# Attention in a hybrid layer: key and query halves through memory, values in two groups, one transpose for the maxima

## The chip, the cores and the metric

The kernel runs on one core of one Trainium2 chip. The metric is the time of one execution in microseconds (us). A core has five engines with a queue each: TensorE (PE, matrix products; its weight loads are shown apart as PEld), VectorE (DVE), ScalarE (ACT), GpSimdE (POOL) and SyncE (SP, which here issues every DMA). Each queue is worked off in order, and an instruction that waits for another engine or a transfer holds back all that stand behind it on its own queue.

## The reference

A layer with three branches (a Fourier mix, a gated delta net, and attention with low-rank queries, keys and values) that are gated, added and projected. The change lies in the third branch alone:

```python
q = (rmsnorm(cq, q_norm) @ w_uq)      # 1024 x 8 heads x (64 + 32 with rope)
kv = (rmsnorm(ckv, kv_norm) @ w_ukv)  # 1280 keys (1024 + 256 context) x 8 x (64 + 64)
s = einsum('bqhd,bkhd->bhqk', q, k) * scale
p = softmax(s, axis=-1)
o = einsum('bhqk,bkhd->bqhd', p, v)   # y_c = o * silu(z)
```

## The kernel before

Products that need full precision take three matmuls: both operands are cut into a rounded high half and a remainder, and hi·hi, hi·lo and lo·hi are added up (mm3, L205 to L207). The program is written in order; a scheduler of the tile framework sets each engine's queue by that order and by its own estimates, and puts in the semaphores. Buffers rotate by name: `st` has three, `s1` two, `ms` one, `pf` ten (PFB).

**qkv** (L1193 on) makes values (`v_tile`), keys (`k_tile`, four head pairs), rotary keys (`k_pe`, which fills the rows 64 to 96 of K00 and K01 with ACT casts L1239 and POOL subtractions L1240, and copies them to K10 and K11 by DMA, L1242/L1243) and queries (`qn_tile`, and `qp_tile` for the rotary part). Keys and queries are stored as whole float32 rows in memory. `load_k` (L1295) and `load_q` (L1303) bring them back in the layout that attention wants, head by head, and cut them there: a cast on ACT (L1300, L1312) and a subtraction on POOL or DVE (L1301, L1313).

**attend** (L1347) has eight blocks j: a head pair (j // 2) times a half of the 1024 queries. A block has 20 weight tiles u: ten key tiles times two heads. `weights` makes three matmuls (L1361 to L1363) into `st`, an exponential on ACT (L1365) and a sum over the keys, kept for the first key tiles on DVE and for the others on POOL (L1374). `values` (L1382) multiplies a weight tile with V; the two heads of a pair use different halves of the array and run side by side. In front of a block stand the maxima of its scores, found while the block before it runs: `peak` makes 20 plain products (L1326, L1331) into `s1`, and DVE reduces each (L1327, L1333). `shift` (L1336) reduces them once more, turns them with eight transposes (L1344) into a row, and ACT copies the row, negated, twice 512 wide, into row 96 of Q (L1345), so that the first matmul of `weights` subtracts the maximum. `finish` (L1389) ends the block before: it adds the two sums of each head (L1394, DVE), a matmul with ones (L1395), a reciprocal 128x512 (L1397), a product with the accumulator (L1398), one with the gate on POOL (L1399), a cast on ACT (L1400) and a subtraction on DVE (L1401). Values come four tiles behind their weights, in five groups per block, but on PE the scheduler parts such groups around other matmuls.

Of the kernel before, what the change touches and what calls it, by code (L numbers as in the profile page):

```python
# [17 lines left out]
P = 128  # L18
L = 1024
# [17 lines left out]
PFB, QB = 10, 3  # L37
AHEAD = 3

# [122 lines left out]
class K:  # L162
    def __init__(self, tc, a, out, dbg=None, stop=None):
        self.tc, self.nc, self.a, self.out = tc, tc.nc, a, out
        self.dbg = dbg or {}
        self.stop = stop
        self.smode = "ad"

# [32 lines left out]
    def mm3(self, out, whi, wlo, rhi, rlo, ks, start=True, stop=True):  # L201
        nc = self.nc
        n = len(ks)
        for j, k in enumerate(ks):
            nc.tensor.matmul(out, whi(k), rhi(k), start=start and j == 0, stop=False)  # L205
            nc.tensor.matmul(out, whi(k), rlo(k), start=False, stop=False)  # L206
            nc.tensor.matmul(out, wlo(k), rhi(k), start=False, stop=stop and j == n - 1)  # L207
# [127 lines left out]
    def prologue(self):  # L335
        nc, tc, a = self.nc, self.tc, self.a
        with ExitStack() as es:
# [7 lines left out]
            def mod_part(s, b):  # L345
# [4 lines left out]
                for kk in range(4):  # L350
                    nc.tensor.transpose(out=ps[:, kk, :], in_=rs[:, kk * P:(kk + 1) * P],
# [28 lines left out]
            for t in range(10):  # L380
                nc.tensor.matmul(ss_ps[:, t:t + 1], acc[:, t * P:(t + 1) * P], self.ones[:, 0:1], start=True, stop=True)
# [3 lines left out]
            for b, n in ((0, 4), (4, 4), (8, 2)):  # L385
                rp = self.g([P, n * P])
                for t in range(n):
# [3 lines left out]
                    nc.tensor.matmul(rp[:, t * P:(t + 1) * P], self.ones, dg, start=True, stop=True)  # L391
# [9 lines left out]
            for i in range(0, ng, 2):  # L401
                m = min(2, ng - i)
                nc.tensor.matmul(pc[i // 2][:, 0:m, :].rearrange("p a (b c) -> p (a b) c", c=P), zr,
                                 zr.unsqueeze(1).broadcast_to([P, 2 * m, P]), start=True, stop=False)
            for k in range(KT):
# [17 lines left out]
                for i in range(ng):  # L423
# [4 lines left out]
                    for ps, rh, rl, first, last in dsts:  # L428
                        nc.tensor.matmul(ps, wh[:, i, :], rh, start=first, stop=False)
                        nc.tensor.matmul(ps, wh[:, i, :], rl, start=False, stop=False)  # L430
                        nc.tensor.matmul(ps, wl[:, i, :], rh, start=False, stop=last and k == KT - 1)
# [5 lines left out]
    def mod_row(self, n, nq, stage):  # L437
# [3 lines left out]
        for q in range(KT):  # L441
# [4 lines left out]
            nc.tensor.matmul(ps, self.sc[:, q, :], wm[:, k * 512:(k + 1) * 512], start=q == 0, stop=q == KT - 1)  # L446
# [19 lines left out]
    def gates_ab(self, smc, sml):  # L466
# [12 lines left out]
        for t in range(10):  # L479
            nc.tensor.transpose(out=ab_ps[:, t, :], in_=(sm[64:80, t * P:(t + 1) * P] if t < 8 else smx[64:80, (t - 8) * P:(t - 7) * P]),  # L480
# [26 lines left out]
        for row, mks in ((0, (MK_LE, MK_GE)), (1, (MK_GT, MK_LT))):  # L507
            for d, g_ in enumerate((gf, gb)):
                nc.tensor.matmul(e_ps[:, row, d * 40:(d + 1) * 40], self.mk[:, mks[d], :], g_, start=True, stop=True)
        nc.tensor.matmul(e_ps[:, 2, :], self.ones, self.gg.rearrange("p d c h -> p (d c h)"), start=True, stop=True)  # L510
# [41 lines left out]
    def k_rows(self, kT, al, tok, ktok, bk, beta, eD):  # L552
# [4 lines left out]
        for b in range(2):  # L557
            tp = al([P, 4, P])
            for u in range(4):
                nc.tensor.transpose(out=tp[:, u, :], in_=tok(kT, 4 * b + u), identity=idn)  # L560
# [15 lines left out]
    def v_rows(self, vT, al, tok, vtok, ivk):  # L576
        nc = self.nc
        idn = self.mk[:, MK_ID, :]
        for b in range(2):
            tp = al([P, 4, P])  # L580
            for u in range(4):
                nc.tensor.transpose(out=tp[:, u, :], in_=tok(vT, 4 * b + u), identity=idn)
# [3 lines left out]
    def lat_load(self, h):  # L586
# [25 lines left out]
        for u in range(8):  # L612
            nc.tensor.matmul(ssq[:, u:u + 1], sqq[:, u * P:(u + 1) * P], self.ones[:, 0:1], start=True, stop=True)
# [3 lines left out]
    def gate_mod(self, c, mp):  # L617
# [15 lines left out]
        nc.tensor.matmul(ps, self.ones[:, 0:1], acc, start=True, stop=True)  # L633
# [3 lines left out]
    def gdn_prep(self, kap, qap, gsl, bsl):  # L637
# [19 lines left out]
        for hf in range(2):  # L657
# [5 lines left out]
            for dr, m_l in enumerate((MK_GT, MK_LT)):  # L663
                nc.tensor.matmul(diff, mk[:, m_l, :], rs[dr], start=dr == 0, stop=dr == 1)
# [3 lines left out]
            for u in range(n):  # L668
                ks = kap(4 * hf + u)
                nc.tensor.matmul(gr[:, u, :], ks, ks, start=True, stop=True)  # L670
# [5 lines left out]
            if qap is not None:  # L676
                gq = self.pp(sh)
                for u in range(n):
                    nc.tensor.matmul(gq[:, u, :], kap(4 * hf + u), qap(4 * hf + u), start=True, stop=True)
# [56 lines left out]
    def invert(self, Y, Z, R):  # L736
# [3 lines left out]
        for i, s in enumerate(LEVELS):  # L740
# [6 lines left out]
            for u in range(n):  # L747
                nc.tensor.matmul(V[:, u, :], Ym[:, u, :], R[:, u, 1, :], start=True, stop=True)
# [14 lines left out]
            for u in range(n):  # L763
                nc.tensor.matmul(AB[:, u, 0, :], L2[:, u, :], R[:, u, 0, :], start=True, stop=True)
            if last:
                break
            for u in range(n):
                nc.tensor.matmul(AB[:, u, 1, :], L3[:, u, :], Vs[:, u, :], start=True, stop=True)
# [28 lines left out]
    def gdn_step(self, st, c, S, kap, ktok, vtok, M, bkc, eg, eL, lat, last, al):  # L797
# [6 lines left out]
        else:  # L804
            a = al([P, 2, P])
            for dr in range(2):
                nc.tensor.matmul(a[:, dr], kap(dr), S[:, dr], start=True, stop=True)
# [4 lines left out]
        for dr in range(2):  # L812
            nc.tensor.matmul(w[:, dr], M(dr), y[:, dr], start=True, stop=True)
        if not last:
# [4 lines left out]
            for dr in range(2):  # L819
                nc.tensor.matmul(sp[:, dr], ktok(dr), u2[:, dr], start=True, stop=True)  # L820
# [9 lines left out]
        if lat is not None:  # L830
# [7 lines left out]
            for dr in range(2):  # L838
                nc.tensor.matmul(oq[:, 2 * dr], qap(dr), S[:, dr], start=True, stop=True)
                nc.tensor.matmul(oq[:, 2 * dr + 1], Qm[:, dr], u1[:, dr], start=True, stop=True)  # L840
# [13 lines left out]
    def gdn_out(self, h, oacc, r):  # L854
# [15 lines left out]
        for b in range(0, 8, 4):  # L870
            tp = self.g([P, 4, P])
            for u in range(4):
                nc.tensor.transpose(out=tp[:, u, :], in_=oacc[:, b + u, :], identity=idn)
# [116 lines left out]
    def spill_in(self, m0, n, dst, mode="copy", ctx=False, ss=None):  # L990
        nc = self.nc
        sq = []
        for m in range(n):
# [23 lines left out]
            if ss is not None and m == n - 1:  # L1017
                nt = w * len(sq) // P
                sp = self.psmm.tile([P, 512], FP32, name="mm", bufs=2)[:, 0:nt]
                for t in range(nt):  # L1020
                    q = sq[t * P // w]
                    b = t * P % w
                    nc.tensor.matmul(sp[:, t:t + 1], q[:, b:b + P], self.ones[:, 0:1], start=True, stop=True)
# [30 lines left out]
    def fourier(self):  # L1054
# [8 lines left out]
        for j in range(2):  # L1063
            ps = self.pp([P, 4, P])
            nc.tensor.matmul(ps.rearrange("p a b -> p (a b)"), dch[:, j, :], fw.rearrange("p a b -> p (a b)"),
                             start=True, stop=True)
            nc.vector.tensor_copy(out=F[:, :, j, :], in_=ps)
        for g in range(4):
# [4 lines left out]
            for t in range(0, 8, 2):  # L1073
                ps = self.g([P, 2, 2 * P])
                for w in range(2):
                    nc.tensor.matmul(ps[:, w], fx[:, (t + w) * P:(t + w + 1) * P],
# [118 lines left out]
    def qkv(self):  # L1195
# [4 lines left out]
        self.knd = dr.tile([4, P, LT], FP32, name="knd")  # L1200
        self.qnd = dr.tile([4, P, L], FP32, name="qnd")
        self.qpd = dr.tile([2, P, L], FP32, name="qpd")
        with ExitStack() as es:
# [42 lines left out]

            def k_tile(t):
# [266 lines left out]
```

## Time and profile before

| | before |
|---|---|
| median of three runs | 1706.43 us (1703.16 to 1708.62) |
| the profiled execution | 1707.65 us, its span 1705.8 us |
| mean granted TensorE clock | 0.957 |
| busy: PE, PEld | 1585.5 us (93%), 1201.4 us (70%) |
| busy: DVE, ACT, POOL | 788.6 us (46%), 558.4 us (33%), 632.3 us (37%) |
| attention, first `st` to the last matmul of ones | 1260.54 to 1548.3 us of the span |

PE is busy nearly all the time, so a time is read as what PE works on, how long each matmul takes at the clock granted in that stretch, and where PE stands still and for whom. In the rows below a number in square brackets is the idle time of the engine ahead of the instruction, and behind the arrow stands what ended it. A matmul's own duration is longer than the distance to the next, since matmuls overlap; the distance is what counts.

### The profile page before, as it was taken

The page shows a single profiled execution, that of the slowest core. Times are in us where ns is not written, and L with a number is a line of the kernel's source. Part 1 is how long each engine was busy: PE and PEld are TensorE (multiplying, and loading weights), DVE is VectorE, ACT ScalarE, POOL GpSimd, SP SyncE. Part 2 cuts the span into 40 slices and gives each one's busy share as a digit, 9 for nine tenths or more (in the row PEclk, how much of TensorE's full clock was granted, in tenths as well). Part 3 has the DMA queues.
Part 4 walks back from the last instruction along what each step waited for, and adds up shares of the span by engine and source line. Part 5 has one row for each costly group of instructions (what it writes and reads, how often), then busy time and mean ns, then how long its engine had stood idle before and what let it go on. Part 6 is the DMA issues. An engine that isn't in the chain of part 4 may idle for free. (4 is left out here: it accounts for less than half of the span.)

```text
span 1705.8 us, 20224 instructions
## 1 busy us (share of the span) xinstructions
PE 1585.5 (93%) x7457; PEld 1201.4 (70%) x7457; DVE 788.6 (46%) x1445; ACT 558.4 (33%) x1145; POOL 632.3 (37%) x500
## 2 busy tenths in 40 slices
PE   6898999999999889998999999999899899999798
PEld 1686888888777777787876788887655445556586
DVE  2755764444343454656445100103365666645522
ACT  3444333322424314343243111212324443333311
POOL 0454242121444354353422222333535654464400
PEclk8889999999999879999999999999979998999999
DMA  8422212211431242313226221315520100004632
GB/s 313 146 60 71 93 62 93 90 63 50 158 94 34 64 82 79 118 68 91 75 64 207 88 68 57 116 59 184 165 75 16 31 16 16 7 7 160 198 99 86
DMA packets 80535, 154.48 MB, mean 91 GB/s; under 512 B 21999, under 2 KB 25743, under 8 KB 80115
## 3 DMA queue, kind: packets, MB, share of 16 engines
q1 hardware_dynamic: 80436, 153.18, 29.0%
q8 instruction: 59, 0.97, 0.3%
q14 instruction: 40, 0.33, 0.1%
HBM read 112.36 MB, written 40.12 MB: 89 GB/s over the span
## 5 line engine op out<-in xcount | busy, mean ns | idle before, releaser
L183 POOL TENSOR_TENSOR wl<-wr,wh 128x512 fp32r<-128x512 f32 (+2 forms) x154 | 209.2, 1360 | 509.0 <-ACT wh L182 495.1
L205 PE MATMUL mm<-hhi,wh 128*128 128x512 f32 x912 | 372.5, 408 | 1.7 <-DVE st L1006 1.3
L207 PE MATMUL mm<-hhi,wl 128*128 128x512 f32 x912 | 367.5, 403 | 0.0
L206 PE MATMUL mm<-hlo,wh 128*128 128x512 f32 x912 | 366.5, 402 | 0.0
L205 PEld LDWEIGHTS mm<-hhi,wh 128*128 128x128 f32 x912 | 175.9, 193 | 38.5 <-issue 2.4
L207 PEld LDWEIGHTS mm<-hhi,wl 128*128 128x128 f32 x912 | 175.3, 192 | 34.5
L206 PEld LDWEIGHTS mm<-hlo,wh 128*128 128x128 f32 x912 | 175.5, 192 | 33.5 <-issue 0.7
L182 ACT CAST wh<-wr 128x512 fp32r<-128x512 f32 (+2 forms) x154 | 93.5, 608 | 253.0 <-PE mm L206 145.8
L1365 ACT ACTIVATE pf<-st 128x512 f32<-128x512 f32 x160 | 94.6, 596 | 137.3 <-PE st L1363 131.8
L1374 POOL TENSOR_TENSOR sum<-sum,pf 128x512 f32<-128x512 f32 x92 | 115.3, 1283 | 49.9 <-ACT pf L1365 49.9
L1327 DVE TENSOR_REDUCE mx<-s 128x1 f32<-128x512 f32 x128 | 85.9, 685 | 35.4 <-PE s L1326 35.1
L1382 PE MATMUL acc<-pf,V 128*64 128x512 f32 x320 | 99.3, 616 | 0.0
L1326 PE MATMUL s<-K,Q 96*128 96x512 f32 x128 | 58.1, 466 | 16.1 <-DVE mx L1327 13.1
L1361 PE MATMUL st<-Q,K 97*128 97x512 f32 x160 | 67.6, 423 | 2.0 <-ACT pf L1365 2.0
L1362 PE MATMUL st<-Q,K 96*128 96x512 f32 x160 | 65.3, 408 | 0.0
L1363 PE MATMUL st<-Q,K 96*128 96x512 f32 x160 | 65.0, 406 | 0.0
L835 POOL TENSOR_TENSOR Qm<-mk,Qf 128x128 f32<-128x128 f32 x64 | 29.6, 482 | 85.5 <-PE g L840 85.5
L1326 PEld LDWEIGHTS s<-K,Q 96*128 96x128 f32 x128 | 25.4, 201 | 48.8 <-DVE mx L1327 27.6
L205 PE MATMUL pf<-woh,mh 128*128 128x512 f32 x128 | 51.2, 400 | 6.0 <-ACT mh L1461 6.0
L1167 DVE SCALAR_TENSOR_TENSOR t<-t,pb 128x1024 f32<-128x1024 f32 x8 | 9.8, 1222 | 95.0 <-PE pb L207 79.2
L1374 POOL TENSOR_TENSOR sum<-pf 128x512 f32<-128x512 f32 x16 | 20.0, 1268 | 89.9 <-ACT pf L1365 69.3
L206 PE MATMUL pb<-yl,wh 128*128 128x512 f32 x128 | 51.2, 400 | 1.2 <-DVE yl L1154 1.2
(395 smaller groups left out, 3023.5 us busy)
## 6 DMA issues: line engine op xcount, KB each, us to landing
wr<-in_win SPq DMA_DIRECT2D x118, 256.0 KB, 2.8
wm<-in_wmod SPq DMA_DIRECT2D x16, 512.0 KB, 6.2
wr<-in_wbr SPq DMA_DIRECT2D x24, 256.0 KB, 2.7
xt<-in_xT SPq DMA_DIRECT2D x8, 640.0 KB, 11.0
wm<-in_win SPq DMA_DIRECT2D x8, 512.0 KB, 4.2
kqd<-lk SPq DMA_DIRECT2D x8, 512.0 KB, 2.6
kqd<-lt SPq DMA_DIRECT2D x8, 512.0 KB, 2.6
tcd<-st SPq DMA_DIRECT2D x16, 256.0 KB, 2.0
```

The source lines that it names most:

```text
L182: nc.scalar.copy(out=hi, in_=raw)
L183: nc.gpsimd.tensor_tensor(out=lo, in0=raw, in1=hi, op=ALU.subtract)
L205: nc.tensor.matmul(out, whi(k), rhi(k), start=start and j == 0, stop=False)
L206: nc.tensor.matmul(out, whi(k), rlo(k), start=False, stop=False)
L207: nc.tensor.matmul(out, wlo(k), rhi(k), start=False, stop=stop and j == n - 1)
L1326: nc.tensor.matmul(ps, q[:, i * P:i * P + P], k[:, 512 * c:512 * c + 512], start=True, stop=True)
L1327: nc.vector.tensor_reduce(out=mx[:, i, c:c + 1], in_=ps, axis=AX.X, op=ALU.max)
L1361: nc.tensor.matmul(ps, kh, qh, start=True, stop=False)
L1362: nc.tensor.matmul(ps, kh[0:KR], ql[0:KR], start=False, stop=False)
L1365: nc.scalar.activation(out=pf, in_=ps, func=AF.Exp)
L1374: eng.tensor_tensor(out=out, in0=s[0], in1=pf, op=ALU.add)
L1382: nc.tensor.matmul(accs[j][64 * par:64 * par + 64], V[:, kt, 64 * h:64 * h + 64], pf, start=kt == 0, stop=kt == 9)
```

## The change

- `put` cuts keys and queries in chunks of 512 columns right behind their products: a cast on ACT, a subtraction on DVE (on POOL for the later query tiles), and one store for each half. `load_k` and `load_q` are then DMAs alone, straight into K and Q.
- Values come in two groups of ten weight tiles, behind u = 1 and u = 11. While `fine` is set, PE's queue keeps the written order. PFB grows from 10 to 16.
- Four peaks come per three weight tiles, so that the last is written at u = 15. The shift comes at u = 17: one transpose of 128x8, one ACT instruction of 8x128, and a DMA of these 4 KB into row 96 of Q.
- `finish` is written in steps over u = 2 to 8, its reciprocal in four quarters.
- In qkv the first block's peaks stand between the query and value tiles, and the second rotary query tile behind the first shift. The sum of its two halves moves from POOL to DVE.

The hunks in which `nc.tensor.matmul` becomes `self.mm` and `nc.tensor.transpose` becomes `self.tr` are left out.

```diff
-PFB, QB = 10, 3
+PFB, QB = 16, 3
 AHEAD = 3
+LAG = (1, 11)
...
+    def mm(self, out, lhsT, rhs, start, stop):
+
+        i = self.nc.tensor.matmul(out, lhsT, rhs, start=start, stop=stop)
+        if self.fine:
+            self.tc.keep_in_program_order(i)
...
+            def put(f, dst, eng):
+
+                for c in range(0, f.shape[1], 512):
+                    e = min(c + 512, f.shape[1])
+                    hi, lo = (up.tile([P, 512], F32R, name=f"cs{l}", bufs=3)[:, 0:e - c] for l in "hl")
+                    nc.scalar.copy(out=hi, in_=f[:, c:e])
+                    eng.tensor_tensor(out=lo, in0=f[:, c:e], in1=hi, op=ALU.subtract)
+                    for d, s in zip(dst, (hi, lo)):
+                        nc.sync.dma_start(out=d[:, c:e], in_=s.bitcast(FP32))
+
             def k_tile(t):
...
-                nc.sync.dma_start(out=self.knd[t], in_=f)
+                put(f, [d[t] for d in self.knd], nc.vector)
...
-                nc.sync.dma_start(out=self.qnd[t], in_=f)
+                put(f, [d[t] for d in self.qnd], nc.gpsimd if t else nc.vector)
...
-                nc.gpsimd.tensor_tensor(out=f, in0=f, in1=g, op=ALU.add)
-                nc.sync.dma_start(out=self.qpd[t], in_=f)
+                nc.vector.tensor_tensor(out=f, in0=f, in1=g, op=ALU.add)
+                put(f, [d[t] for d in self.qpd], nc.gpsimd if t else nc.vector)
...
             for t in range(1, 4):
                 qn_tile(t)
+                peaks(3)
             self.load_q(1)
-            qp_tile(1)
-            self.mx = {}
-            for j in range(20):
-                self.peak(0, j)
             for t in range(VF, 10):
                 v_tile(t)
+                peaks(2)
+            peaks(3)
             self.shift(0)
+            qp_tile(1)

     def load_k(self, t):
-        nc = self.nc
-        f = self.qk.tile([64, 2, LT], FP32, name="kf", bufs=1)
-        nc.sync.dma_start(out=f, in_=self.knd[t].rearrange("(p d) l -> d p l", p=2))
-        kh, kl = (k[0:64] for k in self.Kt[t % 2])
-        nc.scalar.copy(out=kh, in_=f)
-        (nc.gpsimd if t else nc.vector).tensor_tensor(out=kl, in0=f, in1=kh, op=ALU.subtract)
+        for k, src in zip(self.Kt[t % 2], self.knd):
+            self.nc.sync.dma_start(out=k[0:64].bitcast(FP32), in_=src[t].rearrange("(p d) l -> d p l", p=2))
...
-        for par in range(2):
-            ps = self.pss.tile([P, 512], FP32, name="ms", bufs=1)[0:1]
-            for i in range(4):
-                nc.tensor.transpose(out=ps[:, i * P:i * P + P], in_=m4[:, par, i:i + 1], identity=self.mk[:, MK_ID, :])
-            nc.scalar.activation(out=self.Qt[j][0][KR:KR + 1, par, :], in_=ps, func=AF.Copy, scale=-1.0)
+        ps = self.pss.tile([P, 512], FP32, name="ms", bufs=1)[0:8, 0:P]
+        self.tr(out=ps, in_=m4.rearrange("p a b -> p (a b)"), identity=self.mk[:, MK_ID, :])
+        sh = self.qk.tile([8, P], F32R, name="sh", bufs=2)
+        nc.scalar.activation(out=sh, in_=ps, func=AF.Copy, scale=-1.0)
+        nc.sync.dma_start(out=self.Qt[j][0][KR:KR + 1].rearrange("o a (b c) -> o (a b) c", c=P).bitcast(FP32),
+                          in_=sh.bitcast(FP32))
...
                 y = ap.tile([P, 512], FP32, name="yr", bufs=1)
-                nc.vector.reciprocal(out=y, in_=ps)
+                for q in range(4):
+                    qs = slice(q * P, q * P + P)
+                    nc.vector.reciprocal(out=y[:, qs], in_=ps[:, qs])
+                    yield
                 nc.vector.tensor_tensor(out=y, in0=acc, in1=y, op=ALU.mult)
+                yield
...
+                for u in range(20):
+                    todo.append(weights(j, u // 2, u % 2))
+                    while more and n < min(20, (4 * u) // 3 + 1):
                         self.peak(j + 1, n)
                         n += 1
+                    if u in LAG:
+                        for v in todo[:10]:
+                            values(*v)
+                        del todo[:10]
+                    if u == LAG[0] + 1 and j:
+                        ends = finish(j - 1)
+                    if u > LAG[0]:
+                        next(ends, None)
+                    if u == 17 and more:
+                        self.shift(j + 1)
```

On PE, in the middle of a block, the order before parts the values around peaks (`s` with a number is `s1`, `acc` are the values; the line numbers are those of the kernel before):

```order
L1331 MATMUL s_10113<-K_9085,Q_9693 128x256 x2
L1362 MATMUL st<-Q_9495,K_9083 128x512
L1363 MATMUL st<-Q_9495,K_9084 128x512
L1331 MATMUL s_10124<-K_9085,Q_9693 128x256 x2
L1382 MATMUL acc<-pf,V 64x512
L1331 MATMUL s_10135<-K_9085,Q_9693 128x256 x2
L1382 MATMUL acc<-pf,V 64x512 x3
L1331 MATMUL s_10143<-K_9085,Q_9693 128x256 x2
L1361 MATMUL st<-Q_9495,K_9083 128x512
```

The same stretch of PE in the changed kernel, around the second group of values, and with the last peaks ahead of it (every matmul has the line of the wrapper, L173):

```order
L173 MATMUL s_10452<-K_9085,Q_10045 128x512
L173 MATMUL st<-Q_9814,K_9085 128x512
L173 MATMUL st<-Q_9815,K_9085 128x512
L173 MATMUL st<-Q_9814,K_9086 128x512
L173 MATMUL s_10462<-K_9085,Q_10045 128x512
L173 MATMUL acc<-pf,V 64x512 x10
L173 MATMUL st<-Q_9814,K_9085 128x512
L173 MATMUL st<-Q_9815,K_9085 128x512
```

All ten values stand together, behind the peak into s_10462, which takes the buffer of s_10442. On DVE, in the block that this belongs to, the changed kernel has the end of the reciprocal, the product with the accumulator and the last subtraction of `finish` (L1435) between the maxima of those same peaks:

```order
L1429 RECIPROCAL yr<-ms 128x128
L1352 TENSOR_REDUCE mx<-s_10400 128x1
L1352 TENSOR_REDUCE mx<-s_10403 128x1
L1429 RECIPROCAL yr<-ms 128x128
L1352 TENSOR_REDUCE mx<-s_10415 128x1
L1431 TENSOR_TENSOR yr<-acc,yr 128x512
L1352 TENSOR_REDUCE mx<-s_10426 128x1
L1352 TENSOR_REDUCE mx<-s_10439 128x1
L1435 TENSOR_TENSOR y_9805<-zc,y_9801 128x512
L1352 TENSOR_REDUCE mx<-s_10442 128x1
L1352 TENSOR_REDUCE mx<-s_10452 128x1
L1352 TENSOR_REDUCE mx<-s_10462 128x1
```

The maximum of s_10442 stands behind the subtraction into y. On SP, in qkv, the order before is (wr are the query weights, in_wuq; K_9085 and K_9086 are K10 and K11, K_9083 and K_9084 are K00 and K01):

```order
L191 DMA wr<-in_wuq 128x384
L1251 DMA knd<-cst 128x1280
L1235 DMA cst<-kpd 32x1024
L1236 DMA cst<-kped 32x256
L191 DMA wr<-in_wuq 128x384 x2
L1298 DMA kf<-knd 64x2x1280
L1242 DMA K_9085<-K_9083 33x2560
L1243 DMA K_9086<-K_9084 32x2560
L1257 DMA qnd<-cst 128x1024
```

and in the changed kernel:

```order
L1248 DMA cst<-kped 32x256
L1328 DMA K_9083<-knh 64x2x1280
L1328 DMA K_9084<-knl 64x2x1280
L1254 DMA K_9085<-K_9083 33x2560
L1255 DMA K_9086<-K_9084 32x2560
L1267 DMA qnh<-csh 128x512
L1267 DMA qnl<-csl 128x512
L1267 DMA qnh<-csh 128x512
L1267 DMA qnl<-csl 128x512
L204 DMA wr<-in_wuq 128x384 x2
```

Before, five of the eight loads of query weights stand ahead of the two copies of the rotary keys; now one does, and the next two, which the first rotary query tile needs, stand behind the copies and four stores.

## Rows read from the trace of the kernel before

**Rows 1.** Busy time by block of attention: stretch, length, engines, clock, DMA share, GB/s.

```profile
1366.00:1402.00 36.00, 35.45 (x140) 18.58 (x136) 22.52 (x29) 14.97 (x24) 18.58 (x16) 1.00 0.07 19
1402.00:1447.04 45.04, 40.22 (x140) 20.38 (x139) 28.21 (x30) 16.75 (x27) 25.91 (x18) 0.89 0.06 15
...
sum 287.76, PE 274.28 PEld 146.97 DVE 168.80 ACT 116.46 POOL 155.07; mean PE 34.28 PEld 18.37 DVE 21.10 ACT 14.56 POOL 19.38
```

**Rows 2.** PE in order of time, 1379 to 1388: start, length, line, tiles, count.

```profile
1379.85 1.08 PE L1395 MATMUL ms<-sum,ones 128*64 128x512 f32 x4
...
1383.06 0.40 PE L1362 MATMUL st<-Q,K 96*128 96x512 f32 x1
1383.29 0.40 PE L1363 MATMUL st<-Q,K 96*128 96x512 f32 x1
...
1384.31 1.93 PE L1382 MATMUL acc<-pf,V 128*64 128x512 f32 x6
...
1386.60 1.07 PE L1382 MATMUL acc<-pf,V 128*64 128x512 f32 x2
1387.61 0.50 PE L1361 MATMUL st<-Q,K 97*128 97x512 f32 x1
```

**Rows 3.** PE in order of time: transposes, and the idle times of attention.

```profile
1322.03 0.60 PE L1344 MATMUL ms<-mk,m 128*1 128x128 f32 x4
...
1331.47 0.50 PE L1326 MATMUL s<-K,Q 96*128 96x512 f32 x1 [4.06 <-DVE mx L1327]
...
1408.81 0.79 PE L1326 MATMUL s<-K,Q 96*128 96x512 f32 x1 [4.34 <-DVE mx L1327]
...
1538.03 0.50 PE L1361 MATMUL st<-Q,K 97*128 97x512 f32 x1 [2.00 <-ACT pf L1365]
```

**Rows 4.** Costliest groups on the page: the maxima on DVE.

```profile
L1327 DVE TENSOR_REDUCE mx<-s 128x1 f32<-128x512 f32 x128 | 85.9, 685 | 35.4 <-PE s L1326 35.1
```

**Rows 5.** DVE in order of time: one finish, and a sum beside POOL's subtraction.

```profile
1380.98 3.36 DVE L1397 RECIPROCAL yr<-ms 128x512 f32<-128x512 f32 x1 [0.33 <-PE ms L1395]
...
1389.57 0.69 DVE L1401 TENSOR_TENSOR y<-zc,y 128x512 fp32r<-128x512 f32 x1 [2.16 <-ACT y L1400]
...
1402.07 6.08 DVE L1394 TENSOR_TENSOR sum<-sum,sum 128x512 f32<-128x512 f32 x1 [4.68 <-POOL sum L1374]
```

**Rows 6.** POOL and ACT in the same finish.

```profile
1387.59 1.28 POOL L1399 TENSOR_TENSOR zc<-yr,zc 128x512 f32<-128x512 f32 x1
...
1388.91 0.62 ACT L1400 CAST y<-zc 128x512 fp32r<-128x512 f32 x1 [3.90 <-POOL zc L1399]
```

**Rows 7.** DMA issues: KB each, median us to landing.

```profile
zc<-zcd SPq DMA_DIRECT2D x8, 256.0 KB, 2.7
wr<-in_wuq SPq DMA_DIRECT2D x8, 192.0 KB, 3.4
...
yd<-Y SPq DMA_DIRECT2D x40, 8.0 KB, 1.5
```

**Rows 8.** ACT, POOL and PE in qkv, in order of time.

```profile
1201.60 2.42 ACT L1239 CAST K<-cst 32x1280 fp32r<-32x1280 f32 x2
...
1203.44 6.72 POOL L1240 TENSOR_TENSOR K<-cst,K 32x1280 fp32r<-32x1280 f32 x2
...
1204.50 0.51 PE L206 MATMUL st<-cql,wh 128*128 128x512 f32 x1 [0.53 <-DVE cql L1180]
1223.59 0.74 PE L1326 MATMUL s<-K,Q 96*128 96x512 f32 x2 [2.42 <-ACT Q L1312]
1227.44 0.80 PE L205 MATMUL st<-cqh,wh 128*128 128x512 f32 x1 [3.11 <-ACT wh L182]
```

**Rows 9.** Stretches as in rows 1: the first peaks, and two behind idle time.

```profile
1242.77:1260.50 17.73, 14.52 (x34) 6.86 (x33) 15.36 (x24) 2.87 (x4) 5.39 (x4) 0.61 0.32 105
...
1188.57:1192.00 3.43, 3.43 (x9) 2.66 (x9) 2.39 (x4) 1.15 (x1) 0.87 (x1) 0.52 1.02 269
...
1408.80:1420.00 11.20, 11.19 (x28) 6.38 (x29) 6.43 (x10) 2.74 (x5) 0.47 (x1) 0.62 0.15 35
```

More of the change, by code (lines that the diff above doesn't have):

```diff
@@ L380, in prologue @@
             for t in range(10):
-                nc.tensor.matmul(ss_ps[:, t:t + 1], acc[:, t * P:(t + 1) * P], self.ones[:, 0:1], start=True, stop=True)
+                self.mm(ss_ps[:, t:t + 1], acc[:, t * P:(t + 1) * P], self.ones[:, 0:1], start=True, stop=True)
             r10 = xp.tile([P, 10], FP32, name="r10")
@@ L390, in prologue @@
                                             op0=ALU.mult)
-                    nc.tensor.matmul(rp[:, t * P:(t + 1) * P], self.ones, dg, start=True, stop=True)
+                    self.mm(rp[:, t * P:(t + 1) * P], self.ones, dg, start=True, stop=True)
                 nc.scalar.copy(out=rb[:, b * P:(b + n) * P], in_=rp)
@@ L428, in prologue @@
                     for ps, rh, rl, first, last in dsts:
-                        nc.tensor.matmul(ps, wh[:, i, :], rh, start=first, stop=False)
-                        nc.tensor.matmul(ps, wh[:, i, :], rl, start=False, stop=False)
-                        nc.tensor.matmul(ps, wl[:, i, :], rh, start=False, stop=last and k == KT - 1)
+                        self.mm(ps, wh[:, i, :], rh, start=first, stop=False)
+                        self.mm(ps, wh[:, i, :], rl, start=False, stop=False)
+                        self.mm(ps, wl[:, i, :], rh, start=False, stop=last and k == KT - 1)
             nc.sync.dma_start(out=self.mk[:, 1:], in_=a["mk"][:, 1:])
@@ L632, in gate_mod @@
         ps = self.psmm.tile([P, 512], FP32, name="mm", bufs=2)[0:1]
-        nc.tensor.matmul(ps, self.ones[:, 0:1], acc, start=True, stop=True)
+        self.mm(ps, self.ones[:, 0:1], acc, start=True, stop=True)
         nc.vector.scalar_tensor_tensor(out=br, in0=ps, scalar=0.5, in1=br, op0=ALU.mult, op1=ALU.add)
@@ L812, in gdn_step @@
         for dr in range(2):
-            nc.tensor.matmul(w[:, dr], M(dr), y[:, dr], start=True, stop=True)
+            self.mm(w[:, dr], M(dr), y[:, dr], start=True, stop=True)
         if not last:
@@ L1022, in spill_in @@
                     b = t * P % w
-                    nc.tensor.matmul(sp[:, t:t + 1], q[:, b:b + P], self.ones[:, 0:1], start=True, stop=True)
+                    self.mm(sp[:, t:t + 1], q[:, b:b + P], self.ones[:, 0:1], start=True, stop=True)
                 nc.vector.tensor_copy(out=ss[:, 8:10] if ctx else ss[:, 0:8], in_=sp)
@@ L1401, in finish @@
                 nc.vector.tensor_tensor(out=self.ycl[t][:, bs], in0=zc, in1=self.ych[t][:, bs], op=ALU.subtract)
-            last = []
+            self.fine = True
+            todo, ends = [], iter(())
             for j in range(NB):
+                more = j + 1 < NB
                 n = 0
```

118 lines of the change are left out of this document (59 added, 59 removed).

## The prediction

> **What bounds the kernel now.** I read the busy times by block first. In attention PE works 274.28 of 287.76 us, and the next, DVE, 168.80 [rows 1], so PE sets the time and the other engines matter where PE waits for them. The clean block from 1366 runs 36.00 us at full clock; the one from 1402, in which POOL cuts keys, takes 45.04 us at a clock of 0.89 [rows 1]. Then I read PE in order of time. Neighbouring weight matmuls start 0.23 us apart. Two heads' values run side by side: three matmuls (six records) take 1.93 us, so a pair costs about 0.95, but one alone (two records) takes 1.01, as much as a pair [rows 2]. PE's long waits in attention are 4.06 and 4.34 us for DVE's maxima, at the two key loads, and 2.00 us near the end [rows 3]. In the second of them DVE needs 6.08 us for one addition [rows 5], where a like instruction takes 0.69; POOL cuts keys at that time. Behind that wait TensorE was granted 0.62 of full clock for 11.2 us [rows 9].
>
> **Change in attention, PE's own work.** A block with all parts then has 60 weight matmuls, 60 x 0.23 = 13.8; 20 peaks, 4.6, and some 0.4 more for the four that are in halves; two groups of ten values, ten pairs at 0.95 = 9.5; the matmul of ones, 1.0 [rows 2]. The new transpose is not in the trace: at least nothing, at most the 0.60 of the four old ones [rows 3]; I take 0.3. Eight changes of kind at 0.1 (the first matmul behind values shows 0.50 where others show 0.40 [rows 2]) make 0.8. Sum 30.4 us. Against the clean 36.0 that saves three parted groups a block, about one us each, one set of transposes, and some changes of kind.
>
> **DVE in that block.** This is where I expect half the saving to go. Ten values stand at u = 1, and behind them the peaks come at 4/3 per weight tile, with two buffers, so each waits for the maximum two before it. From there to the peak that takes the buffer of s_10442, DVE has 11 maxima at 0.685 = 7.5 [rows 4], two first sums and the products of `finish`, four instructions like the subtraction at 0.69 = 2.8, and the reciprocal, 3.36 in quarters [rows 5]: 13.7 us. The subtraction into y also waits: from the product with the accumulator over POOL 1.28 and ACT 0.62 [rows 6], against two maxima that stand between, 1.4. That is 0.5 us of wait at least; before, it was 2.16 [rows 5], because POOL was in a sum when the product came. It then cost nothing, as few peaks stood right behind; now the maximum of s_10442 does. I take 1.2: 14.9 us. PE's work in the same stretch is 11 peaks 2.5, nine weight tiles 6.2 and the ones 1.1: 9.8 us. PE waits 5.1 us; bounds 3.2 (no wait for POOL, a buffer's lead of one maximum) and 6.2 (wait of 2.2, no lead and 0.3 more for the start of each quarter). The weight tiles in between can't go ahead, as the order is pinned.
>
> **The shift.** The transpose stands at the end of u = 17 and the next block's first weight matmul needs the row. Cover is u = 18 and 19, 6 x 0.23 = 1.4 us. The chain is an exponential ahead on ACT, the small copy and the DMA. No 4 KB DMA is in the trace; the nearest, of 8 KB, lands 1.5 us behind its issue, the 256 KB of the gate take 2.7 [rows 7]. With 1.1 for an exponential and the copy on ACT, each a little below the cast of 0.62 [rows 6], the DMA ends 2.6 to 3.8 us behind the transpose: 1.2 to 2.4 us of wait. I take 1.2, by the small DMA. The Trainium skill ("DMA: Bandwidth & Descriptors", Anatomy of one DMA) puts a fixed cost of about 2 us on a DMA however small; by it the wait would be 1.7, and the six steady blocks 3 us longer together. The row's 1.5 is below that.
>
> **Sum in attention.** A steady block: 30.4 + 5.1 + 1.2 = 36.7, with key loads or without. These no longer hold up DVE, since no cast and no subtraction of keys or queries is left in attention; loads come a block ahead. The first block has 12 values and no `finish`: 13.8 + 5.0 + 5.7 + 0.8 of transpose and changes + 1.2 shift + 2.0 for a slow start and short waits = 28.5. The last has 28 values, two matmuls of ones and no peaks: 13.8 + 13.3 + 2.0 + 0.6 + 2.0 for its last exponential and sums = 31.7. Together 28.5 + 6 x 36.7 + 31.7 = 280.4 against 287.8: -7.4 us. PE still ends last there.
>
> **qkv.** What goes: the waits of 2.42 (for the cast of Q) and 3.11 us (for weights) [rows 8], and the stage of 20 peaks in a row, bound by DVE, 17.7 us to 1260.5 at a mean clock of 0.61 [rows 9]. Half the peaks now stand between products; ten stay behind each other, 10 x 0.69 = 7 us, then transpose, copy and row DMA, 2.8. Saved: 5.5 + 17.7 - 9.8 - 2.3 for the peaks that PE does elsewhere = 11.1, and some 1.4 by the clock: 12.5 us. What comes: 48 stores of halves in place of ten of whole rows, and loads of both halves. These are many more issues on SP, and those of keys stand ahead of the copies of the rotary rows. Above all the weights of the first rotary query tile stand behind K11<-K01. That copy waits for two POOL subtractions, 6.72 us in all, and these for casts of 2.42 us (the first half frees the first subtraction) [rows 8], which now stand behind the cast of the first query tile. PE starts that tile at 1204.5 as before [rows 8] and ends it 18 x 0.23 = 4.1 later; product and cast 1.3, first cast half 1.2, subtractions 6.7, six issues 2, landing 3.4 [rows 7], weight cast 0.5: the weights come 15 us behind PE's last product. PE has nothing else to do in its order there. Behind a shorter wait, that for a product on DVE up to 1188.57, 3.43 us ran at 0.52 of full clock [rows 9]: 1.6 more lost if one such stretch follows. Cost 16.6, so qkv ends 4 us later; bounds -12.5 (no such wait) and +8 (POOL's subtractions slowed by DVE, more stores in the way).
>
> **Sum.** 1707.65 - 7.4 + 4 = 1704.25 us for an execution like the profiled one, which is 1.2 above the median of the runs shown: 1703 us. Behind attention the order is the same, and I count no change.
>
> **Rivals.** (a) TensorE's clock falls in each block. Place: the stretch at u = 2 to 11, where PE now works 9.8 of 14.9 us and has the longest of its waits (over 2 us, for s_10442) at the end. For: the 20 peaks of before, with the same two buffers, ran at 0.61, and lower clock followed the wait of 4.34 us and the shorter one up to 1188.57 [rows 3, 9]. Against: 2.00 us [rows 3] left it at full, and here weight matmuls stand between. Price by the two stretches: 3.43 x 0.48 = 1.6 or 11.2 x 0.38 = 4.3 us a time [rows 9]; with 2.5 in six blocks +15: 1718 us. It decides from 1.5 us a block on: then the time is over 1711.5. The Trainium skill ("TensorE: Matmul & The Clock Gate", A second HAM failure mode: psum-queue depth-cycling) says the like: a kernel that cycles through PSUM buffers with short idle times lets the clock swing between its two levels. The trace agrees for peaks alone (0.61); no row shows it for peaks among weight matmuls.
> (b) DVE's chain costs PE little, because ten waiting values and other weights stand between: a wait of 3.2 or less, -2 in each of six blocks, 1691; with none at all, 1672. For it: in the clean block PE stood still for 0.55 of 36.00 us in all [rows 1], with the same `finish` in it. Against: the peaks stood further apart.
> (c) The rotary copies are ready sooner, and the weights don't wait: 1703 - 16.6 = 1686. Against: POOL and ACT rows give no shorter way.
> That the change does not do what it says (values still parted) I exclude: the order has ten in a row.
>
> **Chances.** Forecast 0.45 (its own range 1694 to 1711), (a) 0.32, (b) 0.12, (c) 0.11. About 5.1 us (0.3%) is what a measurement here tells from no change: faster is below 1701.3, slower above 1711.5. From the forecast 0.40 of its share is faster, 0.52 same, 0.08 slower; of (a) 0.15 same and the rest slower; (b) and (c) are faster. That makes 0.41, 0.28 and 0.31. The range reaches from (c) to a little beyond (a): 1685 to 1721.
>
> **What will show it.** Values as groups of about 4.7 us on PE, twice a block; waits of PE for DVE's maxima of some 5 us a block, the longest near u = 10; a wait near 1.2 us for the row ahead of each block; key-load blocks as long as others; matmul-of-ones intervals near 36.7. In qkv PE stands still some 15 us ahead of the first rotary query tile. The forecast is wrong if the granted clock in attention is below 0.95, if blocks run near 31 us, or if PE goes through qkv without that wait.

## The result

The changed kernel is slower. Its four runs have a median of 1722.88 us (1717.94 to 1727.52) against 1705.02 for the kernel before, a ratio of 1.0096 with a 95% interval of 1.0073 to 1.0118; eleven later runs, in the group of the first experiments, gave 1714.91 (1711.96 to 1726.28) against 1704.23, ratio 1.0055 (1.0034 to 1.0076). The prediction was 1703. The profiled execution took 1717.94 us, its span 1716.2, 10.4 longer than before; it is the fastest of its four.

Where the 10.4 us lie: attention's first weight matmul starts at 1262.83 in place of 1260.54 (+2.3); attention takes 297.3 us in place of 287.8 (+9.5); behind it 1.4 us are gained. The blocks, in the columns of [rows 1], from one block's first weight matmul to the next (the first line starts 1.2 us late):

```profile
1264.00:1302.47 38.47, 29.96 (x106) 18.29 (x104) 16.30 (x24) 14.55 (x26) 21.04 (x17) 0.87 0.22 70
1302.47:1338.73 36.26, 30.94 (x129) 17.57 (x130) 20.77 (x31) 12.49 (x22) 18.73 (x16) 1.00 0.11 29
1338.73:1376.55 37.82, 32.52 (x130) 17.97 (x130) 20.77 (x31) 12.50 (x22) 18.79 (x16) 0.95 0.29 63
1376.55:1415.93 39.38, 34.04 (x130) 18.35 (x130) 20.76 (x31) 12.49 (x22) 18.77 (x16) 0.91 0.10 28
1415.93:1453.88 37.95, 32.63 (x130) 17.98 (x130) 20.76 (x31) 12.49 (x22) 18.76 (x16) 0.96 0.29 63
...
1529.73:1560.10 30.37, 29.98 (x125) 15.53 (x126) 15.98 (x17) 12.56 (x21) 18.17 (x14) 1.00 0.06 19
```

The first block is ten us longer than the 29.7 of before. The six steady blocks together take 227.3 us, as much as before (228.0, key loads and all), though PE's own work fell from 35.4 to 30.9 us in a block at full clock. PE's waits, in the columns of [rows 3] and [rows 8]: the one in qkv, then one steady block and the same peak a block later.

```profile
1221.08 0.80 PE L173 MATMUL st<-cqh,wh 128*128 128x512 f32 x1 [17.16 <-ACT wh L195]
...
1302.47 0.94 PE L173 MATMUL st<-Q,K 97*128 97x512 f32 x3 [1.22 <-DMA Q<-sh]
1311.35 1.08 PE L173 MATMUL ms<-sum,ones 128*64 128x512 f32 x4
1316.14 0.50 PE L173 MATMUL s<-K,Q 96*128 96x512 f32 x1 [0.71 <-DVE mx L1352]
1317.54 0.50 PE L173 MATMUL s<-K,Q 96*128 96x512 f32 x1 [0.19 <-DVE mx L1352]
1320.73 0.50 PE L173 MATMUL s<-K,Q 96*128 96x512 f32 x1 [0.69 <-DVE mx L1352]
1325.36 0.50 PE L173 MATMUL s<-K,Q 96*128 96x512 f32 x1 [2.50 <-DVE mx L1352]
...
1361.63 0.80 PE L173 MATMUL s<-K,Q 96*128 96x512 f32 x1 [2.48 <-DVE mx L1352]
```

Every steady block has these waits: four for maxima, 4.1 us in all, and 1.23 for the row. They differ in what comes behind the longest. At 1325.36 the matmul takes 0.50, at 1361.63 it takes 0.80. The stretches behind three of these waits, as in [rows 9]:

```profile
1325.36:1328.76 3.40, 3.40 (x15) 1.24 (x17) 1.23 (x2) 0.00 (x0) 1.75 (x2) 1.00 0.20 77
1361.63:1365.03 3.40, 3.40 (x9) 1.14 (x11) 1.23 (x2) 0.00 (x0) 1.74 (x2) 0.52 0.25 77
1399.44:1402.84 3.40, 3.40 (x9) 1.11 (x11) 1.24 (x2) 0.00 (x0) 1.75 (x2) 0.50 0.29 80
1402.84:1406.24 3.40, 3.40 (x12) 1.03 (x10) 0.00 (x0) 0.00 (x0) 0.00 (x0) 0.55 0.02 5
```

Behind the first the clock stays at 2.4 GHz and the block takes 36.26 us. Behind the second it is at the lower level, 1.2 GHz, for nearly all of 3.4 us: 3.4 x 0.48 = 1.6 lost, a block of 37.82. Behind the third it stays low twice as long: 3.2 lost, 39.38. Five of six blocks lost something, 9.7 us together.

The subtraction that makes the longest wait, on DVE, POOL and ACT (three views, one stretch), answers [rows 5] and [rows 6]:

```profile
1319.40 0.68 DVE L1431 TENSOR_TENSOR yr<-acc,yr 128x512 f32<-128x512 f32 x1
1319.99 1.28 DVE L1352 TENSOR_REDUCE mx<-s 128x1 f32<-128x512 f32 x2
1324.01 0.69 DVE L1435 TENSOR_TENSOR y<-zc,y 128x512 fp32r<-128x512 f32 x1 [2.74 <-ACT y L1434]
1324.62 1.97 DVE L1352 TENSOR_REDUCE mx<-s 128x1 f32<-128x512 f32 x3
```
```profile
1319.58 2.51 POOL L1400 TENSOR_TENSOR sum<-sum,pf 128x512 f32<-128x512 f32 x2 [0.18 <-ACT pf L1391]
1322.05 1.27 POOL L1433 TENSOR_TENSOR zc<-yr,zc 128x512 f32<-128x512 f32 x1
```
```profile
1323.36 0.62 ACT L1434 CAST y<-zc 128x512 fp32r<-128x512 f32 x1 [3.00 <-POOL zc L1433]
```

The product is ready at 1320.1, POOL is in two sums until 1322.05, and the three maxima behind the subtraction wait with it.

### The profile page after: what moved, and what is told of

Its sections match the earlier page's. It is cut to its first block, busy times and chain, and to the rows that moved or that the text cites. A ratio compares the mean times of both kernels' runs of the same rounds, so it can differ in the third digit from the quotient of the medians.

```text
span 1716.2 us, 20299 instructions
## 1 busy us (share of the span) xinstructions
PE 1554.2 (91%) x7401; PEld 1191.3 (69%) x7401; DVE 780.6 (45%) x1478; ACT 545.8 (32%) x1149; POOL 620.4 (36%) x503
## 5 line engine op out<-in xcount | busy, mean ns | idle before, releaser
L173 PE MATMUL mm<-hhi,wh 128*128 128x512 f32 x912 | 372.2, 408 | 1.7 <-DVE st L1019 1.3
L173 PE MATMUL mm<-hhi,wl 128*128 128x512 f32 x912 | 366.6, 402 | 0.0
L173 PE MATMUL mm<-hlo,wh 128*128 128x512 f32 x912 | 365.2, 400 | 0.0
L173 PEld LDWEIGHTS mm<-hhi,wh 128*128 128x128 f32 x912 | 175.7, 193 | 37.6 <-DVE st L1019 2.2
L173 PEld LDWEIGHTS mm<-hhi,wl 128*128 128x128 f32 x912 | 175.0, 192 | 34.4
L173 PEld LDWEIGHTS mm<-hlo,wh 128*128 128x128 f32 x912 | 175.3, 192 | 33.4 <-issue 0.7
L173 PE MATMUL st<-Q,K 96*128 96x512 f32 (+1 forms) x480 | 138.6, 409 | 8.6 <-DMA Q<-sh 8.6
L173 PEld LDWEIGHTS st<-Q,K 96*128 96x128 f32 (+1 forms) x480 | 88.3, 194 | 46.6 <-issue 19.2
L173 PE MATMUL s<-K,Q 96*128 96x512 f32 (+1 forms) x192 | 68.1, 396 | 29.6 <-DVE mx L1352 29.2
L173 PE MATMUL acc<-pf,V 128*64 128x512 f32 x320 | 83.1, 661 | 3.0 <-ACT pf L1391 3.0
L173 PEld LDWEIGHTS s<-K,Q 96*128 96x128 f32 x192 | 36.1, 193 | 54.3 <-DVE mx L1352 47.6
L173 PEld LDWEIGHTS acc<-pf,V 128*64 128x64 f32 x320 | 23.7, 150 | 52.8 <-issue 48.5
L173 PE MATMUL pf<-woh,mh 128*128 128x512 f32 x128 | 50.7, 396 | 6.0 <-ACT mh L1497 6.0
L1180 DVE SCALAR_TENSOR_TENSOR t<-t,pb 128x1024 f32<-128x1024 f32 x8 | 9.8, 1222 | 93.2 <-PE pb L173 77.3
L173 PE MATMUL pb<-yl,wh 128*128 128x512 f32 x128 | 50.7, 396 | 1.2 <-DVE yl L1167 1.2
L1182 DVE SCALAR_TENSOR_TENSOR t<-t,pb 128x1024 f32<-128x1024 f32 x8 | 9.8, 1220 | 91.5 <-PE pb L173 91.5
```

What stands on the lines that cost most here:

```text
L173: i = self.nc.tensor.matmul(out, lhsT, rhs, start=start, stop=stop)
L1180: nc.vector.scalar_tensor_tensor(out=mg, in0=t, scalar=1.0, in1=ps, op0=ALU.add, op1=ALU.mult)
L1182: nc.vector.scalar_tensor_tensor(out=t, in0=t, scalar=1.0, in1=ps, op0=ALU.add, op1=ALU.mult)
```

## The experiments

All times are medians. Three groups of kernels ran apart, with the kernel before at 1704.23, 1704.67 and 1705.96 us. The part ahead of attention varies by some ten us between executions of any of these kernels: the first query product's second matmul (0.5 us wait for `cql`) starts between 1197.5 and 1208.8. So stretches are counted from there where traces are compared; the changed kernel needs 60.1 us from there to attention and 99.8 to the second block, the kernel before 56.0 and 85.7.

**The changed kernel again** (no edit).

> The changed kernel once more, unaltered. Theory: what differs between its executions is how often TensorE's clock falls behind the 2.5 us wait in a block, 1.5 to 3 us a time; so the time lies between 1716 and 1728 us, the waits of PE are the same to 0.1 us in every block, and a block is either some 36.3 us long (clock 1.00) or 37.8 and more (clock 0.91 to 0.96). Rival: transfers that collide differ from run to run; then the waits themselves differ.

Measured 1714.91 us, just below the 1716 to 1728 expected. The profiled one, 1726.28, has the same waits to 0.03 us in every steady block, and this time all six clocks fall (0.96, 0.96, 0.96, 0.95, 0.95, 0.91 by block; five blocks of 37.8 to 38.0 us and one of 39.4, from first weight matmul to first weight matmul). So these two executions differ by how the clock answers and by the part ahead, not by the waits. The part ahead is the larger: of 8.3 us more than in the first profiled execution, 6.0 lie ahead of the query products and 1.7 in the six blocks.

**Copies of the rotary keys later.** `k_copy()` holds the two lines:

```diff
-                nc.sync.dma_start(out=self.Kt[1][0][64:KR + 1].bitcast(FP32), in_=kh[64:KR + 1].bitcast(FP32))
-                nc.sync.dma_start(out=self.Kt[1][1][64:KR].bitcast(FP32), in_=kl[64:KR].bitcast(FP32))
...
             qp_tile(0)
+            k_copy()
```

> The two copies of the rotary key rows are written behind the first rotary query tile, so that on SP they stand behind its weights. Theory (the weights' place on SP makes the 17.2 us wait): the wait falls to some 8 us (four stores of query halves and the landing are left), and the kernel is 8 to 10 us faster than the changed one, about 1712 to 1715. Rival (the transfers are saturated there, DMA share 0.90, and the weights would be late anyway): the wait stays above 13 us and the time within 4 us of 1722.

Measured 1715.39, no gain. SP in order of time in the changed kernel, where the second copy is issued when POOL's subtractions end (1212.6) and holds up the weights behind it:

```profile
1212.62 0.61 SPq L1255 DMA_DIRECT2D K<-K  x1
...
1216.59 1.41 SPq L204 DMA_DIRECT2D wr<-in_wuq  x2
```

The same with the copies later, and then PE:

```profile
1204.38 1.39 SPq L204 DMA_DIRECT2D wr<-in_wuq  x2
1206.23 0.91 SPq L1259 DMA_DIRECT2D K<-K  x1
```
```profile
1212.60 0.79 PE L173 MATMUL st<-cqh,wh 128*128 128x512 f32 x1 [11.72 <-ACT wh L195]
```

SP now issues the weights ahead of the copies, and the wait falls from 17.2 to 11.7: between the 8 of the theory and the 13 of its rival. These loads land 7.5 us behind their issue, where before the median was 3.4 [rows 7]. The order on SP accounts for 5.5 us of the wait; that the crowd of stores and loads makes much of the rest is argued from these landing times and not shown apart. To the second block the trace gains 3.1 us; the median shows none of it.

**The last cast and subtraction later.**

```diff
+                for _ in range(8):
+                    yield
                 nc.scalar.copy(out=self.ych[t][:, bs], in_=zc)
                 nc.vector.tensor_tensor(out=self.ycl[t][:, bs], in0=zc, in1=self.ych[t][:, bs], op=ALU.subtract)
```

> The cast and the subtraction that end a finish are written eight steps later, so that on DVE the subtraction stands behind the maximum of the peak two before the second group of values, not ahead of it. Theory (the subtraction's wait for POOL and ACT makes PE's 2.5 us wait, and that wait the fall of the clock): the 2.5 us wait is under 0.8, the clock of the six steady blocks is 1.00, blocks take 33.8 to 34.8 us in place of 36.3 to 39.4, and the kernel is 17 to 23 us faster, about 1700 to 1705. Rival (DVE as a whole is the bound, 20.8 us busy in the block): the wait moves to the next peaks, blocks stay over 36 us, the time within 5 us of 1722. Third: the wait goes but the clock still falls, since the many short waits of 0.2 to 0.7 us do it: blocks near 35.5, some 14 us faster.

Measured 1690.53, ratio to before 0.9911 (0.9878 to 0.9944), 24 us faster than the changed kernel, a little more than the 17 to 23 expected. DVE, one steady block:

```profile
1317.73 1.37 DVE L1352 TENSOR_REDUCE mx<-s 128x1 f32<-128x512 f32 x2
1321.17 0.69 DVE L1437 TENSOR_TENSOR y<-zc,y 128x512 fp32r<-128x512 f32 x1 [2.07 <-ACT y L1436]
1321.78 1.28 DVE L1352 TENSOR_REDUCE mx<-s 128x1 f32<-128x512 f32 x2
```

and two blocks by busy time:

```profile
1308.50:1342.00 33.50, 30.69 (x131) 17.60 (x130) 20.76 (x32) 12.50 (x23) 18.81 (x15) 1.00 0.29 63
...
1442.50:1476.01 33.51, 30.69 (x130) 17.58 (x130) 20.76 (x32) 12.51 (x23) 18.80 (x15) 1.00 0.03 9
```

In the order, the subtraction moved behind one maximum more, no further. DVE still waits 2.07 us for it, but the next peak that needs one of the maxima behind it stands behind ten values. The 2.5 us wait is gone from every block, the short ones of 0.69, 0.20 and 0.69 and the 1.23 for the row stay, and the clock is 1.00 in all. So it is not DVE's total, and not the short waits alone. Six blocks of 33.50 against 227.3 are 26.3 us: 2.8 each by the wait itself (36.26 to 33.50), 9.7 by the clock.

**The second rotary query tile early.**

```diff
             self.load_q(1)
+            qp_tile(1)
...
             self.shift(0)
-            qp_tile(1)
```

> The second rotary query tile stands ahead of the last value tiles again, not behind the first shift. Theory (in the first block exponentials stand on ACT behind this tile's casts and behind casts of branch weights, whose loads stand behind its stores on SP; the pinned values and DVE's sums wait for them): the first block, 39.6 us, is under 33, and the kernel some 7 to 10 us faster, about 1713 to 1716. Rival (pinned values behind u = 1 cost that in the first block, whatever stands ahead): it stays above 37 us and the time within 3 us of 1722.

Measured 1711.48, 3.4 us below the changed kernel of the same group, where 7 to 10 were expected. The first block runs from 1268.88 to 1298.86, 30.0 us in place of 39.6, so it is the tile's place. ACT in the changed kernel shows how:

```profile
1265.06 1.14 ACT L1264 CAST csh<-cst 128x512 fp32r<-128x512 f32 x2 [4.88 <-DVE cst L1286]
1266.10 0.59 ACT L1391 ACTIVATE pf<-st 128x512 f32<-128x512 f32 x1
1268.27 0.60 ACT L1391 ACTIVATE pf<-st 128x512 f32<-128x512 f32 x1 [1.58 <-POOL csl L1265]
1271.85 1.28 ACT L195 CAST wh<-wr 128x512 fp32r<-128x512 f32 x2 [2.98 <-DMA wr<-in_wbr]
1273.04 0.59 ACT L1391 ACTIVATE pf<-st 128x512 f32<-128x512 f32 x1
1276.89 0.62 ACT L195 CAST wh<-wr 128x512 fp32r<-128x512 f32 x1 [3.27 <-DMA wr<-in_wbr]
```

The first exponentials stand behind the tile's casts, the next behind casts of branch weights whose loads are late, and PE, at the same time, waits at each:

```profile
1266.74 1.07 PE L173 MATMUL acc<-pf,V 128*64 128x512 f32 x2 [1.88 <-ACT pf L1391]
1268.92 1.59 PE L173 MATMUL acc<-pf,V 128*64 128x512 f32 x2 [1.11 <-ACT pf L1391]
...
1280.06 0.79 PE L173 MATMUL s<-K,Q 96*128 96x512 f32 x1 [3.79 <-DVE mx L1352]
```

Some of it is given back ahead: attention starts 64.1 us behind the query products, 4 later than in the changed kernel, and the second block 94.1, 5.7 earlier. In this execution the clock falls in all six steady blocks, which take 229.0 us, 1.7 more than in the first one.

**The shift one weight tile earlier, or two later**, both with the late cast; the first edit, the other has 19.

```diff
-                    if u == 17 and more:
+                    if u == 16 and more:
```

> As the one with the late cast, and the shift one weight tile earlier, at u = 16, so that three weight tiles (2.1 us) cover the row's way and not two (1.4 us). Theory (the row's chain takes a fixed 2.6 us or so): the wait of 1.23 us ahead of each block falls to some 0.5 us, steady blocks 32.8 us, the kernel about 5 us faster than with the late cast alone, 1685 to 1687. Rival (the transpose itself then waits for the last maximum on DVE): no gain, within 2 us.

> As the one with the late cast, and the shift two weight tiles later, at u = 19, which takes its cover away: PE then waits some 2.6 us for the row, once a block, with PE fully busy before and behind. Theory (a single wait over 2.4 us or so is enough for the clock to fall): the clock is below 0.97 in the steady blocks, which take 36 to 38 us, and the kernel is 17 us or more slower than with the late cast alone. Rival (the clock fell in the changed kernel because the whole stretch ahead of the wait, with its short waits, left PE under-used): the clock stays at 1.00, blocks take 34.9 us, and it is 8 to 11 us slower.

At u = 16: 1687.98 us, 2.6 below the late cast alone, in separate groups. The wait for the row is 0.16 to 0.28 in place of 1.23, but the transpose now waits 0.30 for the last maximum; blocks take 32.9, so 0.6 us is gained in each, near the 0.7 expected; the time gained is half of the 5 us expected. At u = 19: 1727.07, ratio 1.0141 (1.0110 to 1.0171). The expected wait of 2.6 us, 2.7 measured, is there only ahead of the last two blocks; ahead of the other five it is 3.6 to 6.0, and a lower clock follows each of these. Three of the waits, on PE:

```profile
1344.75 1.62 PE L173 MATMUL st<-Q,K 97*128 97x512 f32 x3 [5.61 <-DMA Q<-sh]
...
1498.86 0.94 PE L173 MATMUL st<-Q,K 97*128 97x512 f32 x3 [2.69 <-DMA Q<-sh]
...
1533.78 1.40 PE L173 MATMUL st<-Q,K 97*128 97x512 f32 x5 [2.67 <-DMA Q<-sh]
```

SP ahead of the first shows why: the row now stands behind a load of keys.

```profile
1338.82 0.58 SPq L1328 DMA_DIRECT2D K<-knh  x1
1339.89 0.69 SPq L1370 DMA_DIRECT2D Q<-sh  x1
```

From 1339.89 it took 4.9 us to PE's start; in the changed kernel, with nothing ahead (issued at 1300.54), 1.9. On the theory of the clock this one is inconclusive: of the two single waits of 2.7 us one left it at full and one did not, as the stretches behind them show.

```profile
1498.90:1503.00 4.10, 4.10 (x18) 2.14 (x20) 3.57 (x4) 1.19 (x2) 1.75 (x2) 1.00 0.00 0
...
1533.80:1537.80 4.00, 4.00 (x12) 1.77 (x14) 2.36 (x2) 1.19 (x2) 1.78 (x2) 0.67 0.00 0
```

**Three changes together**: late cast, shift at u = 16, rotary tile early; the edits are those three diffs.

> The late cast, the shift at u = 16 and the second rotary query tile ahead of the value tiles, together. If the three act apart from each other, the times add: 5 us by the shift and 3 us by the tile below the late cast alone, about 1682 us. If the first block's waits only hide others, the tile brings nothing: 1686.

Measured 1683.46 us (1676.25 to 1685.23), ratio to before 0.9872 (0.9839 to 0.9905): the best of all, and below both kernels. The times add, near the 1682 expected. The first block and a steady one:

```profile
1266.94:1296.10 29.16, 28.71 (x109) 17.39 (x110) 14.63 (x23) 13.18 (x24) 17.85 (x14) 0.91 0.18 59
1304.99:1337.85 32.86, 30.83 (x130) 17.51 (x129) 20.75 (x32) 12.58 (x23) 18.78 (x15) 1.00 0.27 60
```

**Attention alone**: the kernel before up to `load_q`, and from `peak` on the changed one with the late cast; then keys split ahead, and the shift at u = 16, in two more.

```diff
 # attention alone: qkv, load_k and load_q as before the change
-                put(f, [d[t] for d in self.knd], nc.vector)
+                nc.sync.dma_start(out=self.knd[t], in_=f)
 # keys ahead: that, u == 16, and for keys alone put, the plain load_k, and k_copy
-                nc.sync.dma_start(out=self.knd[t], in_=f)
+                put(f, [d[t] for d in self.knd], nc.vector)
```

> Attention of the changed kernel with the late cast, but keys and queries stored whole and cut when they are loaded, as in the kernel before, and its order in qkv. Theory (the splitting ahead costs in qkv and in the first block about what it saves in the key-load blocks): attention starts some 3 us earlier than with the late cast, the first block takes 29 to 31 us in place of 40, the three blocks in which keys are cut take 37 to 40, and the kernel is within 6 us of the late cast's 1690. Rival (without it, casts of keys and queries hold up exponentials and DVE in a pinned order): the steady blocks are over 36 us on the mean and the kernel over 1700 us.

> Attention alone with the late cast and the shift at u = 16, but keys (not queries) are split right behind their products, with the copies of the rotary key rows behind the first rotary query tile. Theory (splitting keys ahead frees the key-load blocks, 12 us, and it is the stores of query halves and the moved query tile that cost in qkv and the first block): all steady blocks 32.8 to 33.5 us at full clock, the first block 29 to 31, the wait for the first rotary query tile's weights under 9 us, and the kernel at 1671 to 1679 us, below the three changes together. Rival (the stores of key halves and their place ahead of the weights make the wait): the wait is over 12 us, qkv ends 6 us or more later than without them, and the kernel is at 1681 to 1688.

> Attention alone with the late cast and the shift at u = 16: keys and queries are stored whole and cut when loaded. The comparison for splitting keys ahead. If the shift acts here as with the split halves, 5 us below the 1690 without it: 1684 to 1686 us; waits of some 3.6 us for DVE's maxima stay in the two blocks in which POOL cuts keys.

Attention alone: 1689.67 us, the same as the late cast with the halves. Attention starts 56.9 us behind the query products (3.2 sooner) and the first block takes 29.8 (10 less). POOL cuts keys in two blocks, not in the three expected (another cut stands in qkv); these two, and the ones behind them, cost that again: 38.51, 34.68, 38.18 and 35.20 between matmuls of ones, 12.6 more than four of 33.5. The wait there, on PE, then DVE and POOL at that time:

```profile
1328.66 0.80 PE L173 MATMUL s<-K,Q 96*128 96x512 f32 x1 [3.62 <-DVE mx L1340]
```
```profile
1319.71 6.09 DVE L1409 TENSOR_TENSOR sum<-sum,sum 128x512 f32<-128x512 f32 x1 [5.29 <-POOL sum L1388]
```
```profile
1319.64 5.61 POOL L1314 TENSOR_TENSOR K<-kf,K 64x2560 fp32r<-64x2560 f32 x1
```

With keys split ahead, 1688.40; without, 1689.09, both with the shift at u = 16, which here brought less than 1 us, not the 5 expected. Splitting keys ahead made all steady blocks 32.9 us, as its theory said, but the time is the rival's: PE waits 12.06 us in qkv, and attention starts 68.7 us behind the query products, against 57.5 without.

## Why the prediction was wrong

**What held.** PE's work in a steady block: 30.4 predicted, 30.7 to 30.9 measured at full clock. The wait for the row: 1.2, and 1.23 measured, but in part by luck. From the end of the transpose to the issue took 0.7 us where 1.1 was counted, from the issue to PE's start 1.9 where 1.5 was:

```profile
1299.57 0.28 PE L178 MATMUL ms<-mk,m 128*8 128x128 f32 x1
```
```profile
1300.54 0.68 SPq L1370 DMA_DIRECT2D Q<-sh  x1
```

The waits for maxima: 5.1, and 4.1, with the longest at the peak named, for the buffer of s_10442. The upper bound of 6.2 for them does not come out of its terms: 5.1, 1.0 more of wait and 0.3 make 6.4, and 7.3 if each of the four quarters adds its 0.3. The last block: 31.7 and 30.4. qkv: 4 us late, and 60.1 - 56.0 = 4.1 measured, with the wait at 17.2 where 15 was counted and the gains, by what is left over, larger by as much; that the two misses cancel is luck. The path of the wait was as predicted, the weights behind a copy that waits for POOL, but it is not the whole reason: with the copies moved, 11.7 us stayed.

**What failed.** First, the choice of full clock for six blocks in the sum. Rival (a) had 0.32 and 2.5 us a block; it happened in five of six blocks, with 1.6 or 3.2 us, 9.7 in all, so blocks that would be 36.3 took 37.9 on the mean. The late cast shows its cause: with the 2.5 us wait, and only that, taken away, the clock was 1.00 throughout. The forecast counted that wait and its length, and had a row of a like wait (up to 1188.57) with half clock behind it, but followed the single row of 2.00 us that left the clock alone. That like wait was 2.37 us long, nearer to the 2.5, and PE had no wait in the 20 us ahead of it:

```profile
1188.57 0.64 PE L205 MATMUL st<-ckh,wh 128*128 128x512 f32 x1 [2.37 <-DVE cst L1250]
```

So this row had the fall without short waits ahead; whether they make it more likely stays open, as the two single waits of 2.7 us at u = 19 went either way. The Trainium skill ("TensorE: Matmul & The Clock Gate", A second HAM failure mode: psum-queue depth-cycling) says that short waits at PSUM buffers can make the clock swing. The runs agree as far as the swing goes; but short waits alone, of 0.2 to 0.7 us, left the clock at full here.

Second, the step "2.0 for a slow start and short waits" in the first block: 28.5 predicted, 39.6 measured, 11 us, the largest single miss. The prediction did not follow the second rotary query tile, moved behind the first shift, on any queue. On ACT its casts, the branch weights' casts and the first exponentials stand in one line; PE's waits of 1.9, 1.1 and 3.8 us come from that, the last one by way of DVE's sums, and the clock of the block is 0.87. The fourth experiment shows that it is the tile's place: moved ahead, the block takes 30.0.

Third, a size: the subtraction's wait, 1.2 predicted with 2.2 as the bound, was 2.74, since POOL was in two sums, not one, when the product came. The smaller waits were over-counted by more, so the sum for the waits came out 1 us high; yet this size made the one wait at which the clock fell.

Together: attention 280.4 predicted, 297.3 measured. Of the 16.9, 11.1 is the first block, 7.1 the steady blocks (9.7 of clock less 2.6, since waits were 1.0 smaller and PE's work 0.5 larger in each), -1.3 the last. Against the 1704.25 forecast for an execution like the profiled one, 1717.94 is 13.7 more: these 16.9, less 1.8 ahead of the query products, a part that varies by more than that from one execution to the next, and 1.4 behind attention. The measured median lies another 5 us above the profiled run; the other three executions have a lower mean clock (0.949 to 0.954 against 0.957), but no trace says in which stretch.

## What to carry to other kernels

A wait of two or three microseconds on a busy TensorE can cost double, since the clock may fall behind it (here 2.5 us of wait, and 1.6 or 3.2 more by the clock); so a pinned order should put the one late instruction behind work that nobody waits for, which took one moved cast and subtraction here (24 us). Where a step is moved, its instructions are to be followed on every engine's queue, ACT's too: casts that wait for a load hold up the exponentials behind them. Work taken out of a loop and put ahead of it is gained only if what stands ahead has room: the splitting of keys and queries, with the order of qkv that came with it, cost as much in qkv and in the first block as it saved. With the rotary tile early it seems to gain some 5 us (1683.46 against 1689.09, in separate groups, with ratios to before whose intervals overlap), so that is not shown.

## What was not expected of the hardware

- A wait of 2.5 us, with shorter ones ahead, was followed by a lower clock in 23 of 24 steady blocks (four profiled executions with the same waits), though the waits agree to some hundredths of a microsecond; the loss came in about two sizes, 1.6 and 3.2 us. Of single waits, 2.00 us left the clock at full, 2.37 did not, and 2.7 did in one of two cases.
- A DMA of 4 KB needed 1.9 us from its issue to the matmul that it released with nothing ahead, 2.8 to 2.9 us when a load of queries had been issued some 1.1 us earlier on the same queue, and 4.9 to 5.3 us when that was a load of keys (at u = 19). The 8 KB row of before gave 1.5 [rows 7]. The Trainium skill ("DMA: Bandwidth & Descriptors", Anatomy of one DMA) gives a fixed cost of about 2 us, which was nearer; that section describes DMAs issued by GpSimd, and SyncE issues these.
- An addition on DVE beside POOL's subtraction of keys took 6.09 us with attention alone, as before (6.08 [rows 5]), where a product of the same size on DVE takes 0.68.
